# Where a group's sums of squares and its first output pieces stand among the projections: a Mamba-2 / HGRN2 trunk on one Trainium2 core

## The chip, the core and the metric

The program runs on one core of one Trainium2 chip. The metric is device time in microseconds (us). The core has five engines with a queue each: TensorE (PE in the profile, its weight loads PEld), VectorE (DVE), ScalarE (ACT), GpSimd (POOL) and SyncE (SP, which here only issues transfers). An engine takes its instructions in the order of its queue; engines wait for each other by semaphores.

## The reference, cut to what matters

Two layers on 512 tokens of width 1024. The first one's token mixer is a Mamba-2 SSD, and the change lies in it. Its last steps are a gated output, a norm over each of 4 groups of 512 channels, and a projection:

```python
zxbcdt = u @ w_in
xbc = silu(causal_depthwise_conv(xbc, conv_w, conv_b))
...
y = y_diag + y_off + d_skip * xs
y = y.reshape(bsz, seq, SSD_D_INNER) * silu(z)
y = rms_norm(y.reshape(bsz, seq, g_, SSD_D_INNER // g_), norm_w)
return y.reshape(bsz, seq, SSD_D_INNER) @ w_out
```

What follows (layer norm, squared-ReLU MLP, a gated embedding, then the second layer with an HGRN2 mixer) is not touched.

## The kernel before, in words

Products in float32 are made of three float32r products each: every operand is split into a high part (`whi`, a cast on ScalarE, `L110`) and a low part (`wlo`, a subtraction on VectorE, `L112`), and `mm3` (`L116` to `L118`) adds high x high, low x high and high x low. A weight unit of 128 x 1024 is loaded into one of 3 buffers `raw`, then split into one of 6 buffers `whi` and one of 6 `wlo`; so the cast of a later unit waits until TensorE has done with the unit that had its buffer.

The 2048 channels of the SSD are 16 tiles of 128 channels, 4 to a group. `x_part(j)` projects tile j (24 matmuls into a bank of PSUM), and `conv_silu` makes `xs` of it: a start on ScalarE (`L570`), three steps on VectorE (`L573`), silu on ScalarE (`L574`). `z_part(j)` projects its gate and applies silu (`L622`). `decays`, `states`, `turn_pair` and `mixed` are the scan: decay products `m` (`L663`, exp `L668`, product with `cbm` `L669`) and `cd` (`L656`), a pair's states by matmul (`L679`), a pair's transposes (`L639`), and the output `py` (`L696`, `L698`). `finish(j, ...)` gates the output, splits it into `ys[g]` and adds its square to `ss[g]` (`L724`).

A loop over rounds k = 1 to 8 takes the tiles in pairs. Round k projects tiles 2k and 2k+1 and mixes the pair before, 2k-2 and 2k-1. So group 0's fourth square is added at the end of round 2, group 1's in round 4, group 2's in round 6. In rounds 3, 5 and 7 `rms_group` sums the squares over the channels with four float32 matmuls against a matrix of 1/512 (`L729`, the sums), takes the root on ScalarE (`L731`) and the reciprocal on VectorE (`L732`): `ri`. The group's part of the output projection comes in 8 pieces of 12 matmuls (`out_part`, 4 token chunks by 2 halves of the width); VectorE scales a piece by `ri` and adds it to `acc` (`L250`). `some(n)` puts the next n pieces into the queue, and the table `PIECES` says how many stand in a round before its second projection (`mine`) and how many behind it (`theirs`). Group 2's pieces come in round 8.

TensorE's order is the order of the code (`manual_schedule`). The orders of the other queues are made by a scheduler when the program is built, from the same code and its priorities. Four banks of PSUM (`psj`, `pj` in names) go round among projections, sums and pieces: a matmul that is the first to write a bank waits until its last reader is done.

Of the kernel before, what the change touches and what calls it, by code (L numbers as in the profile page):

```python
# [41 lines left out]
def trunk(ctx: ExitStack, tc, a):  # L42
# [11 lines left out]
    psj = pool("psj", 4, space=PSUM)  # L54
# [10 lines left out]
    def mk(p, shape, tag, dt=F32, **kw):  # L65
        return p.tile(list(shape), dt, tag=tag, name=nm(tag), **kw)
# [22 lines left out]
    def bank(p, tag):  # L89
        return mk(p, [P, T], tag)  # L90
# [8 lines left out]
    def unit(src, lead=LEAD):  # L99
        n = src.shape[1]  # L100
        with tc.high_priority(offset=lead):
            raw = mk(raws, [P, 1024], "raw")
            nc.sync.dma_start(raw[:, :n], src)
        return split(raw[:, :n], lead)
# [133 lines left out]
    def out_part(units, n, xs, c, h, first, scale, last=False, sums=None):  # L238


        sl = slice(c * P, (c + 1) * P)
        ps = bank(psj, "pj")
        for k in range(n):
            hi, lo = units[k // 2]
            ks = slice((k % 2) * 512, (k % 2 + 1) * 512)
            mm3(ps, xs.h(k, sl), xs.l(k, sl), hi[:, ks], lo[:, ks], k == 0, k == n - 1)
        d = acc[:, c, h * 512 : (h + 1) * 512]
        with tc.high_priority(offset=SOON if last else 0):
            if scale is not None:
                nc.vector.scalar_tensor_tensor(d, ps, scale[:, c : c + 1], d, ALU.mult, ALU.add)  # L250
            elif sums is not None:
                nc.vector.tensor_tensor_reduce(d, ps, d, 1.0, 0.0, ALU.add, ALU.add, sums[:, c, h : h + 1])
            elif first:
                nc.vector.scalar_tensor_tensor(d, d, ALPHA, ps, ALU.mult, ALU.add)
            else:
                nc.vector.tensor_add(d, ps, d)
# [301 lines left out]
    def dt_tail():  # L558

        pt = bank(psm, "pm")  # L560
        for i, src in enumerate((dt, wt, cs)):
            nc.tensor.transpose(pt[:, i * P : (i + 1) * P], src, ident)
        t = mk(cpool, [P, 3, NCH, 32], "toks")
        nc.vector.tensor_copy(t, pt[:, : 3 * P].rearrange("p (i c h) -> p i c h", i=3, c=NCH))
        return [t[:, i] for i in range(3)]
# [20 lines left out]
    def bc_group(g):  # L586
        bcm = []
        for which in range(2):
            ps = projected(10 * g + which)
            t = tmp(("bm", "cm")[which], [P, T])  # L590
            conv_silu(ps, 16 + 4 * which + g, t)
            bcm.append(t)
        return bcm

    def bc_prep(bcm, pt, pc):
        bm, cm = bcm
        for c in range(3):
            nc.tensor.transpose(pt[:, c * P : (c + 1) * P], bm[:, c * P : (c + 1) * P], ident)
        btok = tmp("btok", [P, 3, P])
        nc.scalar.copy(btok, pt[:, : 3 * P].rearrange("p (c n) -> p c n", c=3))  # L600
        for c in range(NCH):
            sl = slice(c * P, (c + 1) * P)
            nc.tensor.matmul(pc[:, sl], bm[:, sl], cm[:, sl], start=True, stop=True)
        cbm = tmp("cbm", [P, T])
        nc.vector.tensor_mul(
            cbm.rearrange("p (c l) -> p c l", c=NCH), pc.rearrange("p (c l) -> p c l", c=NCH), bc(triu, 1, NCH)
        )
        return btok, cbm, cm
# [4 lines left out]
    def x_part(j):  # L613
        ps = projected(10 * (j // 4) + 2 + 2 * (j % 4))
        xs = tmp("xs", [P, T])
        conv_silu(ps, j, xs)
        live[j] = [xs]

    def z_part(j):
        ps = projected(10 * (j // 4) + 3 + 2 * (j % 4))  # L620
        sz = tmp("sz", [P, T])
        nc.scalar.activation(sz, ps, AF.Silu)  # L622
        if j in live:
            live[j].insert(1, sz)
        return sz

    def load_decay(j):
        csb = mk(w4, [P, 2, T], "a")
        nc.sync.dma_start(csb, bass.AP(tensor=csd.tensor, offset=csd.offset + 2 * j * T, ap=[[0, P], [T, 2], [1, T]]))
        decay[j] = csb  # L630

    def turn_pair(k, pts):
        dt_tok, w_tok, cs_tok = toks
        xw = tmp("xw", [P, 3, 2, 2, 64])
        pair[k] = [xw, mk(sm, [P, 2, 2, NCH], "cd")]
        for t, pt in enumerate(pts):
            xs = live[2 * k + t][0]
            for c in range(NCH):
                nc.tensor.transpose(pt[:, c * P : (c + 1) * P], xs[:, c * P : (c + 1) * P], ident)  # L639
        views = [pt.rearrange("p (c h q) -> p c h q", c=NCH, h=2) for pt in pts]  # L640
        for t, v in enumerate(views):
            j = 2 * k + t
            nc.vector.tensor_mul(xw[:, :, t], v[:, 0:3], bc(w_tok[:, 0:3, 2 * j : 2 * j + 2], 3, 64))
        for t, v in enumerate(views):
            j = 2 * k + t
            xdt = tmp("xdt", [P, NCH, 2, 64])
            nc.vector.tensor_mul(xdt, v, bc(dt_tok[:, :, 2 * j : 2 * j + 2], 3, 64))
            live[j].append(xdt)
# [77 lines left out]
    def rms_group(g, pr):  # L726

        for c in range(NCH):
            nc.tensor.matmul(pr[:, 64 * c : 64 * c + 64], ss[g][:, c * P : (c + 1) * P], ones_s, start=True, stop=True)  # L729
        ri = mk(sm, [P, NCH], "ri")  # L730
        nc.scalar.activation(ri, pr[:, : 64 * NCH].rearrange("p (c n) -> p c n", c=NCH)[:, :, 0], AF.Sqrt, bias=eps)  # L731
        nc.vector.reciprocal(ri, ri)  # L732
        return ri

    def pieces(g, ri):

        for h in range(2):
            units = [unit(a["wso"][4 * g + 2 * h + i]) for i in range(2)]
            for c in range(NCH):
                out_part(units, 4, ys[g], c, h, False, ri)  # L740
                yield

    outs = iter(())
    bcm = {}

    def some(n):
        for _ in range(n):
            next(outs)

    PIECES = {3: (2, 2), 4: (2, 2), 5: (2, 2), 6: (2, 2)}  # L750

    with tc.manual_schedule(engines={mybir.EngineType.PE}):
        bcm[0] = bc_group(0)
        for j in range(2):
            load_decay(j)
            x_part(j)
            z_part(j)
        prep[0] = bc_prep(bcm[0], bank(pst, "pt"), bank(psy, "py0"))
        toks.extend(dt_tail())
        turn_pair(0, (bank(psy, "py1"), bank(psj, "pj")))  # L760
        for k in range(1, 9):
            i, j = 2 * k, 2 * k + 1
            mine, theirs = PIECES.get(k, (0, 0))
            decays(i - 2)
            if k < 8:
                if k in (4, 6):
                    bcm[k // 2] = bc_group(k // 2)
                x_part(i)
            else:
                finish(13, *held[:2], z_part(13))  # L770
                z_part(14)
            states(k - 1)
            if k in (3, 5, 7):
                outs = pieces(k // 2 - 1, rms_group(k // 2 - 1, bank(psj, "pj")))
            decays(i - 1)
            some(mine)
            if k < 8:
                load_decay(i)
                x_part(j)
                load_decay(j)  # L780
            some(theirs)
            if k == 1:
                bcm[1] = bc_group(1)
            elif k < 7:
                z_part(i - 2)
                z_part(i - 1)
            elif k == 7:
                z_part(12)
            else:
                z_part(15)  # L790
                some(4)
            if k == 2:
                nc.sync.dma_start(acc, a["x"])
                for c in range(NCH):
                    nc.vector.tensor_scalar(acc[:, c, :], acc[:, c, :], ALPHA, None, ALU.mult)
            done = [mixed(i - 2), (mixed(i - 1))] if k != 7 else [mixed(12)]
            if k == 7:
                live[13].insert(1, None)
                held = mixed(13)
            if k < 8:  # L800
                if k % 2 == 0:
                    prep[k // 2] = bc_prep(bcm[k // 2], bank(psj, "pj"), bank(psj, "pj"))
                turn_pair(k, (bank(pst, "pt"), bank(psm, "pm")))
            for t, d in enumerate(done):
                finish(i - 2 + t, *d)
        some(4)
# [494 lines left out]
```

## Time and profile before

| | us |
|---|---|
| timed runs | 1434.31, 1432.96, 1432.22; median 1432.96 |
| the profiled execution | 1434.46 |
| its span on the core | 1432.4 |
| TensorE busy | 1417.2 (99%) |
| VectorE, ScalarE busy | 1023.5 (71%), 738.7 (52%) |
| TensorE waiting for VectorE's `L724` before `L729` | 6.9 in 3 waits |

A row of the timeline gives start, length, engine, line, operation, out<-in, shapes, how many instructions it merges, and in brackets the idle time before it with what ended it. A float32 matmul stands there as two records, so the four matmuls of the sums are x8. PEclk in a row of a stretch is the clock that TensorE was granted, 1.00 for full speed. The profiled execution's own time is 2.06 us more than its span.

### The profile page before, as it was taken

How to read it: one execution, taken by the hardware profiler on the slowest of the kernel's cores; microseconds unless marked ns; L12 is line 12 of the kernel's file. 1: busy time of each engine (PE TensorE's matmuls, PEld its weight loads, DVE VectorE, ACT ScalarE, POOL GpSimd, SP SyncE). 2: the span in 40 equal slices, each digit the busy share in tenths (PEclk: the TensorE clock that was granted, in tenths of full speed). 3: DMA queues.
4: the chain of work that ended last, by engine and by line, in shares of the span. 5: the costliest groups of instructions: out<-in, count | busy, mean ns of one | idle time of the engine just before them, and what ended most of it. 6: DMA issues, size and time to landing. Idle time of an engine off the chain costs nothing.

```text
span 1432.4 us, 20277 instructions
## 1 busy us (share of the span) xinstructions
PE 1417.2 (99%) x8063; PEld 1183.9 (83%) x8063; DVE 1023.5 (71%) x1673; ACT 738.7 (52%) x1085; POOL 1.6 (0%) x9
## 2 busy tenths in 40 slices
PE   9999999999999999999999999999999999999998
PEld 7887878878888888888888888888898888888887
DVE  7996876696966768676874674766795867667873
ACT  7884655574255454445543445464455454543641
POOL 0000000000000000000000000000000000000000
PEclk9999999999999999999999999999999999999999
DMA  7423223322533444443422232222163444434231
GB/s 289 169 98 103 104 90 117 108 98 104 177 117 118 147 132 147 140 140 131 134 95 84 75 103 90 79 85 90 47 244 107 147 135 145 147 132 162 89 118 44
DMA packets 48958, 174.81 MB, mean 122 GB/s; under 512 B 5728, under 2 KB 6368, under 8 KB 48736
## 3 DMA queue, kind: packets, MB, share of 16 engines
q1 hardware_dynamic: 48864, 173.52, 35.6%
q8 instruction: 63, 1.03, 0.3%
q14 instruction: 31, 0.25, 0.1%
HBM read 171.34 MB, written 2.16 MB: 121 GB/s over the span
## 4 chain that ended last, share of the span: by engine, by line
PE 92%; DVE 5%; ACT 1%; DMA 1%; issue 0%; SPq 0%; ACTq 0%
PE pj L116 24%; PE pj L117 24%; PE pj L118 24%; PE py L116 5%; PE py L117 5%; PE py L118 5%; PE py L960 1%; PE py L696 1%; DMA acc<-in_x 1%; DVE wlo L112 1%; PE py L698 0%; PE pt L230 0%; DMA acc<-in_xw 0%; PE pm L230 0%; ACT whi L110 0%
## 5 line engine op out<-in xcount | busy, mean ns | idle before, releaser
L110 ACT CAST whi<-raw 128x1024 fp32r<-128x1024 f32 x226 | 237.1, 1051 | 404.0 <-PE pj L117 277.6
L112 DVE TENSOR_TENSOR wlo<-raw,whi 128x1024 fp32r<-128x1024 f32 x226 | 275.0, 1221 | 206.6 <-ACT whi L110 200.6
L116 PE MATMUL pj<-b,whi 128*128 128x512 f32 (+1 forms) x1008 | 380.5, 378 | 0.2 <-ACT b L235 0.2
L117 PE MATMUL pj<-b,whi 128*128 128x512 f32 (+1 forms) x1008 | 378.9, 376 | 0.7 <-DVE b L236 0.7
L118 PE MATMUL pj<-b,wlo 128*128 128x512 f32 (+1 forms) x1008 | 378.7, 376 | 0.0
L118 PE MATMUL pj<-whi,b 128*128 128x512 f32 (+1 forms) x592 | 230.2, 389 | 0.0
L116 PE MATMUL pj<-whi,b 128*128 128x512 f32 (+1 forms) x584 | 229.8, 394 | 0.1
L117 PE MATMUL pj<-wlo,b 128*128 128x512 f32 (+1 forms) x584 | 227.0, 389 | 0.0
L117 PEld LDWEIGHTS pj<-b,whi 128*128 128x128 f32 x1008 | 189.7, 188 | 34.8 <-DVE b L236 0.9
L118 PEld LDWEIGHTS pj<-b,wlo 128*128 128x128 f32 x1008 | 189.7, 188 | 34.7
L116 PEld LDWEIGHTS pj<-b,whi 128*128 128x128 f32 x1008 | 189.5, 188 | 34.7 <-ACT b L235 0.5
L118 PEld LDWEIGHTS pj<-whi,b 128*128 128x128 f32 x592 | 111.8, 189 | 22.9 <-DVE b L1155 0.2
L116 PEld LDWEIGHTS pj<-whi,b 128*128 128x128 f32 x584 | 110.5, 189 | 23.3 <-ACT k L889 0.5
L117 PEld LDWEIGHTS pj<-wlo,b 128*128 128x128 f32 x584 | 110.5, 189 | 21.6
L110 ACT CAST whi<-r 128x1024 fp32r<-128x1024 f32 x64 | 67.1, 1049 | 65.0 <-PE pj L118 36.8
L112 DVE TENSOR_TENSOR wlo<-r,whi 128x1024 fp32r<-128x1024 f32 x64 | 78.1, 1220 | 21.8 <-ACT whi L110 21.8
L118 PE MATMUL py<-whi,b 128*128 128x512 f32 x216 | 84.1, 390 | 0.0
L117 PE MATMUL py<-wlo,b 128*128 128x512 f32 x192 | 74.7, 389 | 0.0
L116 PE MATMUL py<-whi,b 128*128 128x512 f32 x192 | 74.4, 389 | 0.0
L573 DVE SCALAR_TENSOR_TENSOR cv<-pj,cst,cv 128x509 f32<-128x509 f32 (+2 forms) x66 | 48.9, 743 | 2.8 <-ACT cv L570 2.4
L118 PEld LDWEIGHTS py<-whi,b 128*128 128x128 f32 x216 | 40.5, 188 | 8.5
L116 PEld LDWEIGHTS py<-whi,b 128*128 128x128 f32 x192 | 36.0, 188 | 7.6
(335 smaller groups left out, 1808.0 us busy)
## 6 DMA issues: line engine op xcount, KB each, us to landing
raw<-in_w SPq DMA_DIRECT2D x112, 512.0 KB, 3.3
r<-in_w SPq DMA_DIRECT2D x64, 512.0 KB, 3.4
raw<-in_wssd SPq DMA_DIRECT2D x38, 512.0 KB, 4.0
a<-csd SPq DMA_DIRECT2D x16, 512.0 KB, 3.6
raw<-in_wso SPq DMA_DIRECT2D x16, 512.0 KB, 3.4
raw<-in_wg SPq DMA_DIRECT2D x16, 512.0 KB, 3.3
raw<-in_whvg SPq DMA_DIRECT2D x16, 512.0 KB, 3.4
raw<-in_whq SPq DMA_DIRECT2D x16, 512.0 KB, 3.3
```

Source lines behind the costliest of these rows:

```text
L110: nc.scalar.copy(hi[:, :n], f)
L112: nc.vector.tensor_sub(lo[:, :n], f, f32(hi[:, :n]))
L116: nc.tensor.matmul(out, sh, mh, start=start, stop=False, **kw)
L117: nc.tensor.matmul(out, sh, ml, start=False, stop=False, **kw)
L118: nc.tensor.matmul(out, sl, mh, start=False, stop=stop, **kw)
L573: nc.vector.scalar_tensor_tensor(cv[:, d:], ps[:, : T - d], convw[:, i, k : k + 1], cv[:, d:], ALU.mult, ALU.add)
L696: nc.tensor.matmul(yd[64 * r : 64 * r + 64, sl], xdt[:, c, r, :], m[:, r, sl], start=True, stop=c == 0)
L960: nc.tensor.matmul(ps[r][32 * b : 32 * b + 32, base + n * c : base + n * c + n], kk[r][:, ts], moving(r, 4 * c + b), start=True, stop=True,)
```

## The change

The sums and the iterator over the pieces are made behind the second projection of rounds 3, 5 and 7 instead of behind `states`, and in rounds 3 and 5 the table puts four pieces behind that projection and none before it. Rounds 4 and 6 keep two and two, round 8 is as it was.

```diff
-    PIECES = {3: (2, 2), 4: (2, 2), 5: (2, 2), 6: (2, 2)}
+    PIECES = {3: (0, 4), 4: (2, 2), 5: (0, 4), 6: (2, 2)}
...
             states(k - 1)
-            if k in (3, 5, 7):
-                outs = pieces(k // 2 - 1, rms_group(k // 2 - 1, bank(psj, "pj")))
             decays(i - 1)
             some(mine)
             if k < 8:
                 load_decay(i)
                 x_part(j)
                 load_decay(j)
+            if k in (3, 5, 7):
+                outs = pieces(k // 2 - 1, rms_group(k // 2 - 1, bank(psj, "pj")))
             some(theirs)
```

On TensorE in round 3, before: the states of pair 2 (`pt`, `pm`), the sums into `pj_1078`, and the first piece into `pj_1112`, whose stationary operand `b` is the gated output `ys`.

```order
L679 MATMUL pt_1067<-xw_981,btok_971 128x256 x2
L679 MATMUL pm_1068<-xw_981,btok_971 128x256
L729 MATMUL pj_1078<-ones_s_169,ss_734 128x64 x4
L116 MATMUL pj_1112<-whi_1102,b_115_727 128x512
L117 MATMUL pj_1112<-wlo_1104,b_115_727 128x512
L118 MATMUL pj_1112<-whi_1102,b_116_728 128x512
```

And now, the same place in the code's order of sums and first piece: the last matmuls of the second projection (tile 7, `pj_1094`), the sums into `pj_1134`, and the first piece into `pj_1154`.

```order
L116 MATMUL pj_1094<-b_6_112,whi_1097 128x512
L117 MATMUL pj_1094<-b_8_114,whi_1097 128x512
L118 MATMUL pj_1094<-b_6_112,wlo_1099 128x512
L729 MATMUL pj_1134<-ones_s_169,ss_734 128x64 x4
L116 MATMUL pj_1154<-whi_1144,b_115_727 128x512
L117 MATMUL pj_1154<-wlo_1146,b_115_727 128x512
L118 MATMUL pj_1154<-whi_1144,b_116_728 128x512
```

The sums no longer follow the float32 matmuls of the states; they stand between float32r matmuls on both sides, and the projection follows the states. Three pieces (`pj_1168`, `pj_1182`, `pj_1196`) follow the first one. In the built program the second waits for the last convolution step of the first projection, the third for the root (`L731`), the fourth for the last convolution step of the second projection.

On ScalarE in round 3, before, behind the square of tile 3 (`sq_1010`): the root `ri`, the silu of tile 6 (`xs_1060`), an exp, `cd`, the cast of a later weight unit (`whi_1398`) and the convolution's start of tile 7 (`cv_1174`).

```order
L720 ACTIVATE sq_1010<-y_1005 128x512
L731 ACT_TABLE_LOAD
L731 ACTIVATE ri_1083<-pj_1078,cst_165 128x4
L574 ACT_TABLE_LOAD
L574 ACTIVATE xs_1060<-cv_1061 128x512
L668 ACT_TABLE_LOAD
L668 ACTIVATE b_1086<-b_1086 128x1024
L656 ACTIVATE cd_1309<-a_1180 128x8
L110 CAST whi_1398<-raw_1396 128x1024
L570 ACTIVATE cv_1174<-pj_1142,cst_165 128x512
```

And now, where tile 7's convolution is `cv_1126`:

```order
L720 ACTIVATE sq_1010<-y_1005 128x512
L110 CAST whi_1398<-raw_1396 128x1024
L570 ACTIVATE cv_1126<-pj_1094,cst_165 128x512
L574 ACT_TABLE_LOAD
L574 ACTIVATE xs_1060<-cv_1061 128x512
L668 ACT_TABLE_LOAD
L668 ACTIVATE b_1078<-b_1078 128x1024
L731 ACT_TABLE_LOAD
L731 ACTIVATE ri_1139<-pj_1134,cst_165 128x4
L656 ACT_TABLE_LOAD
L656 ACTIVATE cd_1309<-a_1132 128x8
```

The root went from first to behind the cast, the convolution's start, silu and exp. The cast waits for the second projection's last matmul with a high weight, because `whi_1398` takes the buffer of `whi_1097`. In round 5 the order is the same but for the convolution's start, which stands behind the exp.

On ScalarE in round 7, before, from the exp to the silu of the second projection's tile, 15 (`xs_2605`); `sz_2645` is the gate of tile 12:

```order
L668 ACTIVATE b_2558<-b_2558 128x1024
L570 ACTIVATE cv_2606<-pj_2574,cst_165 128x512
L656 ACTIVATE cd_2680<-a_2612 128x8
L110 CAST whi_2860<-raw_2858 128x1024
L110 CAST whi_2968<-raw_2966 128x1024
L622 ACT_TABLE_LOAD
L622 ACTIVATE sz_2645<-pj_2614 128x512
L574 ACTIVATE xs_2605<-cv_2606 128x512
```

And now, where it is `xs_2597`; the cast `whi_2860`, the silu of tile 14 and its table load, and the exp's table load stand ahead of the first row:

```order
L668 ACTIVATE b_2550<-b_2550 128x1024
L570 ACTIVATE cv_2598<-pj_2566,cst_165 128x512
L731 ACT_TABLE_LOAD
L731 ACTIVATE ri_2611<-pj_2606,cst_165 128x4
L622 ACT_TABLE_LOAD
L622 ACTIVATE sz_2645<-pj_2614 128x512
L656 ACT_TABLE_LOAD
L656 ACTIVATE cd_2680<-a_2604 128x8
L574 ACT_TABLE_LOAD
L574 ACTIVATE xs_2597<-cv_2598 128x512
```

The root and three table loads came between exp and that silu. On TensorE, `L639` transposes `xs_2597` behind the mixing of tiles 12 and 13.

## Prediction

> **What bounds the kernel now.** I read the page first, then TensorE's waits, then the stretches around each wait with the granted clock. TensorE is busy for 99% of the span, and in the SSD stage it waits for one thing only: `L729`, the matmuls that add up a group's sums of squares. The columns of the wait are total us, times, longest.
>
> ```profile
> PE 1417.2 (99%) x8063; PEld 1183.9 (83%) x8063; DVE 1023.5 (71%) x1673; ACT 738.7 (52%) x1085; POOL 1.6 (0%) x9
> ```
> ```profile
> PE pj L729 <- DVE ss L724: 6.9, 3, 3.0
> ```
>
> Next, six of the stretches of 3.41 us: start and end, length, busy time of TensorE, weight loads, VectorE, ScalarE and GpSimd, then PEclk.
>
> ```profile
> 108.34:111.75 3.41, 1.48 (x11) 1.42 (x12) 3.41 (x8) 1.87 (x3) 0.00 (x0) 1.00 0.00 0
> 111.75:115.16 3.41, 3.41 (x10) 2.63 (x9) 3.41 (x12) 2.09 (x3) 0.00 (x0) 0.51 0.00 0
> ...
> 200.49:203.90 3.41, 1.45 (x9) 0.97 (x7) 3.41 (x8) 3.39 (x5) 0.00 (x0) 1.00 0.00 0
> 203.90:207.31 3.41, 3.41 (x13) 2.93 (x13) 3.41 (x11) 1.39 (x3) 0.00 (x0) 0.51 0.00 0
> ...
> 292.64:296.05 3.41, 2.17 (x10) 1.51 (x8) 3.41 (x7) 2.73 (x4) 0.00 (x0) 1.00 0.00 0
> 296.05:299.46 3.41, 2.69 (x16) 2.39 (x17) 3.41 (x8) 1.68 (x3) 0.00 (x0) 1.00 0.00 0
> ```
>
> A wait costs more than its length here. After a stretch in which TensorE was busy for 1.48 or 1.45 us, the next stretch ran at 0.51; after 2.17 and 2.69 it did not. The two lowered stretches lie 92.15 us apart, 27 times 3.413, so I read them as steps of one fixed grid: a grid step with 1.93 us or more of idleness costs half the clock for the next step, one with up to 1.24 us costs nothing. A lowered step costs 3.41 x 0.49 = about 1.65 us.
>
> **What is removed.** TensorE's rows at the three places, from the last states matmul to the first matmul behind the moved work (start, length, line; 129.17, 222.44 and 312.84 start a z projection). In round 3:
>
> ```profile
> 106.69 0.59 PE L679 MATMUL pm<-xw,btok 128*128 128x256 f32 x2
> 110.27 1.08 PE L729 MATMUL pj<-ones_s,ss 128*128 128x64 f32 x8 [2.98 <-DVE ss L724]
> 111.15 0.48 PE L116 MATMUL pj<-whi,b 128*128 128x512 f32 x1
> 111.47 0.39 PE L117 MATMUL pj<-wlo,b 128*128 128x512 f32 x1
> ...
> 123.73 0.39 PE L116 MATMUL pj<-whi,b 128*128 128x512 f32 x1
> ...
> 129.17 0.39 PE L116 MATMUL pj<-b,whi 128*128 128x512 f32 x1
> ```
>
> In rounds 5 and 7:
>
> ```profile
> 200.95 0.59 PE L679 MATMUL pm<-xw,btok 128*128 128x256 f32 x2
> 203.50 1.57 PE L729 MATMUL pj<-ones_s,ss 128*128 128x64 f32 x8 [1.96 <-DVE ss L724]
> ...
> 222.44 0.39 PE L116 MATMUL pj<-b,whi 128*128 128x512 f32 x1
> ```
> ```profile
> 294.21 0.59 PE L679 MATMUL pm<-xw,btok 128*128 128x256 f32 x2
> 296.77 1.10 PE L729 MATMUL pj<-ones_s,ss 128*128 128x64 f32 x8 [1.96 <-DVE ss L724]
> 297.68 0.47 PE L116 MATMUL pj<-b,whi 128*128 128x512 f32 x1
> ...
> 303.25 0.39 PE L116 MATMUL pj<-b,whi 128*128 128x512 f32 x1
> ...
> 308.78 0.66 PE L696 MATMUL py<-b,xdt 128*64 128x128 f32 x8
> ...
> 311.99 0.66 PE L639 MATMUL pt<-cst,xs 128*128 128x128 f32 x4
> 312.48 0.60 PE L639 MATMUL pm<-cst,xs 128*128 128x128 f32 x4
> 312.84 0.48 PE L116 MATMUL pj<-b,whi 128*128 128x512 f32 x1
> ```
>
> Before therefore spends 22.48 us (129.17 - 106.69), 21.49 us and 18.63 us there.
>
> **What after spends, on TensorE alone.** A projection straight behind states is in round 1, where no sums stand between:
>
> ```profile
> 78.11 0.59 PE L679 MATMUL pm<-xw,btok 128*128 128x256 f32 x2
> 78.35 0.58 PE L116 MATMUL pj<-b,whi 128*128 128x512 f32 x1
> ...
> 84.00 0.39 PE L116 MATMUL pj<-b,whi 128*128 128x512 f32 x1
> ```
>
> So the second projection starts 0.24 us behind states and takes 5.65 us. The sums have had their data by 110.27, 203.50 and 296.77 (their starts now); in after their turn comes at 106.69 + 5.89 = 112.58, at 206.84 and at 300.10, so the old waits go. The sums take 0.88 us (110.27 to 111.15), two pieces 5.44 us (123.73 to 129.17), so 2.72 each, and the first matmul behind the sums 0.09 us more than the usual 0.23. This is also the cost of the "run of their own": the projection behind states starts slowly (0.2 us), as the one behind the sums did before, and both are in these rows. Rounds 3 and 5, without any new wait: 0.24 + 5.65 + 0.88 + 0.09 + 4 x 2.72 = 17.74 us.
>
> What else moves is hidden: on SyncE's queue the second projection's weight load changes places with the pieces' two, three slots for the same three loads in their order of use, all cast a round ahead; GpSimd's queue is the same. On ScalarE the new order alternates functions more often and has one table load more in rounds 3 and 5 each and two in round 7.
>
> **The new wait of rounds 3 and 5.** Four pieces in a row need four of the pool's four banks. In the built program the third piece waits for ScalarE's square root, which reads the bank of the sums, and the fourth for the second projection's third convolution step on VectorE. ScalarE's queue there (its order in round 3 above): the cast of a weight unit into the second projection's buffer, the convolution's start, then a table load and silu, a table load and exp, a table load and the square root. Before, the square root was first. The prices:
>
> ```profile
> 111.38 0.26 ACT L731 ACTIVATE ri<-pj,cst 128x4 f32<-128x4 f32 x1 [1.42 <-PE pj L729]
> 113.04 1.28 ACT L574 ACT_TABLE_LOAD   x1 [1.39 <-DVE ri L732]
> ...
> 116.27 1.06 ACT L668 ACTIVATE b<-b 128x1024 f32<-128x1024 f32 x1
> ...
> 123.70 1.05 ACT L110 CAST whi<-raw 128x1024 fp32r<-128x1024 f32 x1 [5.41 <-PE pj L117]
> 124.66 0.78 ACT L570 ACTIVATE cv<-pj,cst 128x512 f32<-128x512 f32 x1
> ```
>
> The cast started 0.03 us before the projection's successor (123.73), so call the projection's end E: cast and convolution start end at E + 1.71 (123.70 to 125.44), table load to end of exp takes 4.29 (113.04 to 117.33), table load and square root 1.28 + 0.26, gaps 0.05: E + 7.6. TensorE stands before the third piece at E + 0.88 + 2.81 + 2.72 = E + 6.41. A wait of 1.2 us, in both rounds. At under 1.24 us it leaves the clock alone by the rows. The fourth piece: exp ends at E + 6.0, then VectorE runs one m product, one convolution step, the reciprocal, one weight subtraction and the last step:
>
> ```profile
> 119.16 1.21 DVE L669 TENSOR_TENSOR b<-b,cbm 128x1024 f32<-128x1024 f32 x1
> 120.29 1.22 DVE L112 TENSOR_TENSOR wlo<-raw,whi 128x1024 fp32r<-128x1024 f32 x1
> ...
> 127.32 1.53 DVE L573 SCALAR_TENSOR_TENSOR cv<-pj,cst,cv 128x510 f32<-128x510 f32 x2
> ```
>
> 1.2 + 1.2 + 1.5 + 0.1 = 4.0 at most, E + 10.0; the fourth piece stands at E + 7.6 + 2.72 = E + 10.3. Covered, barely; if the subtraction slips, it costs that much. Round 3: 22.48 - 17.74 - 1.2 = 3.5 us gained. Round 5: 21.49 - 18.94 = 2.5 us.
>
> **The new wait of round 7.** No pieces follow; behind the sums come one z projection (5.57, 297.68 to 303.25, and 0.1 into the mixing), two mixings (3.21, 308.78 to 311.99) and the first half of the turn (0.49). The second half transposes what silu makes of the second projection. That projection starts 3.2 us earlier than before (294.21 + 0.24 = 294.45 for 297.68), but in ScalarE's order of round 7 the root and three table loads now come between the exp and this silu. The missing prices:
>
> ```profile
> 304.91 0.21 ACT L656 ACTIVATE cd<-a 128x8 f32<-128x8 f32 x1 [0.18 <-DMA a<-csd]
> ...
> 311.02 0.60 ACT L622 ACTIVATE sz<-pj 128x512 f32<-128x512 f32 x1
> 311.51 0.62 ACT L574 ACTIVATE xs<-cv 128x512 f32<-128x512 f32 x1
> ```
>
> With E = 300.10: cast to E + 1.0, table load to exp E + 5.3, convolution start E + 6.0, table load and square root E + 7.5, table load and z silu E + 9.4, table load and cd E + 10.9, table load and silu E + 12.8 = 312.9. TensorE is there at E + 0.88 + 5.67 + 3.21 + 0.49 = 310.35. A wait of 2.6 to 2.7 us, and the z projection starts 0.36 us later (312.48 to 312.84), at 313.4 instead of 312.84: 0.6 us lost, the old wait of 2.2 and more exchanged for a later one.
>
> **The clock.** The 2.5 us of idleness in round 7 lies on an unknown phase of the grid. If 1.93 us in one step are needed, 60% of the phases give them (27% have no boundary inside, and 46% of the rest leave a part that long); if just over 1.24 are enough, all do. I take a lowered step, 1.6 us. [...]
>
> **Sum.** 3.5 + 2.5 - 0.6 - 1.6 = 3.8 us off the profiled execution's 1434.46, 1430.7. Behind this stage TensorE has no wait above 1 us, so I carry the gain to the end. The profiled execution stands 1.5 us above the runs' median of 1432.96. That may be the profiling (then 1429.2 for a median run) or one lowered step that a median run doesn't pay (then 1430.7); I take 1429.9.
>
> **Rivals.** A, the forecast, 1429.2 to 1430.7: 45%. B, the round-7 wait lowers no step, for its phase on the grid or because short gaps don't lower it as a rule: 1.6 less, 1427.6 to 1429.1: 20%. [...] C, ScalarE gets through faster than I walked it and no new wait appears: 1.2 + 1.2 + 2.7 + 1.6 less, 1422.5 to 1424.0: 6%; against it, each load in the queue has its row. D, the new waits are longer by a few tenths, so each of the three holds enough idleness and lowers the clock: 1434.46 - 5.4 + 4.9 = 1434.0, or 1432.5 on the median's scale, no change: 20%. E, slower: the row of four runs out of banks, and the third piece waits until VectorE has emptied the first (behind the last convolution step, about E + 10.6 instead of E + 7.6). Then rounds 3 and 5 wait 3.0 us more each, 6.0, and three steps are lowered: 1434.46 - 5.4 + 6.0 + 4.9 = 1440.0, or 1438.5. It decides as soon as that bank is the one handed out; for it speaks that VectorE was busy through 3.41 of 3.41 us in the quoted stretches, against it that the program's waits name the square root. With any other backlog of that size: 9%.
>
> 0.2% of the time, 2.9 us, is about what a measurement of this kernel can tell from no change: faster means below 1430.1, slower above 1435.8. A is split 25 to 20 by that line: faster 25 + 20 + 6 = 51%, same 20 + 20 = 40%, slower 9%. The range leaves out C, E and a few per cent at B's and D's far ends: 1427.0 to 1434.0.
>
> **What would show it.** Right: no TensorE wait at `L729`; waits of 1.0 to 1.3 us at the third piece (`L116`) of rounds 3 and 5, released by ScalarE `L731`; one of about 2.5 us at `L639` in round 7, released by ScalarE `L574`; at most one step at 0.51. Wrong: a wait left at `L729` (the sums' data come later than now), waits released by VectorE `L573` or `L250` at the pieces, or new waits outside the SSD stage.

## The result, and the profile after

| | before | after |
| --- | --- | --- |
| median, us | 1434.65 (8 runs, 1432.22 to 1435.57) | 1429.88 (8 runs, 1428.67 to 1430.94) |
| profiled execution, us | 1434.46 | 1430.54 |
| its span, us | 1432.4 | 1428.5 |

The ratio after to before is 0.9969 (95% interval 0.9959 to 0.9978). That is faster by 0.3%: small, but the interval leaves out 1. The three runs of before in the first table were on the low side: with the five taken beside the changed kernel the median is 1434.65, close to the profiled execution.

TensorE's waits of the changed kernel (total us, times, longest):

```profile
PE pm L639 <- ACT xs L574: 2.7, 1, 2.7
PE pj L116 <- ACT ri L731: 2.2, 2, 1.1
```

`L729`, which led this view before with 6.9 us, is gone. In its place stand the two new waits: the third piece twice, the second half of round 7's turn once. 6.9 us of waits became 4.9.

TensorE's rows at the three places (start, length, line), from the last states matmul to the first matmul behind the moved work. Rounds 3 and 5:

```profile
106.13 0.59 PE L679 MATMUL pm<-xw,btok 128*128 128x256 f32 x2
112.03 1.00 PE L729 MATMUL pj<-ones_s,ss 128*128 128x64 f32 x8
112.84 0.48 PE L116 MATMUL pj<-whi,b 128*128 128x512 f32 x1
119.68 0.50 PE L116 MATMUL pj<-whi,b 128*128 128x512 f32 x1 [1.12 <-ACT ri L731]
125.25 0.39 PE L116 MATMUL pj<-b,whi 128*128 128x512 f32 x1
```
```profile
197.03 0.59 PE L679 MATMUL pm<-xw,btok 128*128 128x256 f32 x2
210.56 0.50 PE L116 MATMUL pj<-whi,b 128*128 128x512 f32 x1 [1.10 <-ACT ri L731]
216.17 0.39 PE L116 MATMUL pj<-b,whi 128*128 128x512 f32 x1
```

The sums now start without a wait, and so do the first, second and fourth piece; the third waits 1.12 and 1.10 us. States to z projection takes 19.12 us (125.25 - 106.13) and 19.14 us, where it took 22.48 and 21.49.

Round 7:

```profile
287.95 0.59 PE L679 MATMUL pm<-xw,btok 128*128 128x256 f32 x2
...
306.86 0.66 PE L639 MATMUL pm<-cst,xs 128*128 128x128 f32 x4 [2.69 <-ACT xs L574]
307.27 0.48 PE L116 MATMUL pj<-b,whi 128*128 128x512 f32 x1
```

From states to the z projection it takes 19.32 us now and took 18.63: 0.69 us lost. And the wait of 2.69 us has a consequence, which the stretches around it show (start and end, length, busy time of TensorE, weight loads, VectorE, ScalarE and GpSimd, PEclk):

```profile
304.40:307.90 3.50, 1.04 (x7) 0.95 (x8) 3.46 (x14) 3.46 (x6) 0.00 (x0) 1.00 0.00 0
307.90:311.30 3.40, 3.40 (x10) 2.64 (x9) 3.40 (x8) 3.37 (x5) 0.00 (x0) 0.51 0.06 18
```

The clock in the second stretch is 0.51: one lowered step behind the wait. No stretch of rounds 3 and 5 of this profile is below 1.00.

The two profiles can now be closed against each other. TensorE reaches round 3 0.56 us earlier than before (106.13 for 106.69), a difference that arose ahead of all changed code: it is there already behind the states of round 1 (77.55 for 78.11). Then 22.48 - 19.12 = 3.36 and 21.49 - 19.14 = 2.35 are gained, 0.69 and one step of 3.41 x 0.49 = 1.65 lost: 0.56 + 3.36 + 2.35 - 0.69 - 1.65 = 3.93 us. The spans differ by 3.9 us. Nothing behind round 7 gives any of it back.

### The profile page after: what moved, and what is told of

The parts are those of the page before. It is cut to its first block, busy times and chain, and to the rows that moved or that the text cites. A ratio compares the mean times of both kernels' runs of the same rounds, so it can differ in the third digit from the quotient of the medians.

```text
span 1428.5 us, 20283 instructions
## 1 busy us (share of the span) xinstructions
PE 1415.3 (99%) x8063; PEld 1182.2 (83%) x8063; DVE 1023.1 (72%) x1673; ACT 743.9 (52%) x1089; POOL 1.6 (0%) x9
## 4 chain that ended last, share of the span: by engine, by line
PE 93%; DVE 3%; ACT 2%; DMA 1%; issue 0%; SPq 0%; DVEq 0%; ACTq 0%
PE pj L116 24%; PE pj L117 24%; PE pj L118 24%; PE py L116 5%; PE py L117 5%; PE py L118 5%; PE py L696 1%; PE py L960 1%; DVE wlo L112 1%; PE py L698 1%; DMA a<-csd 1%; PE pt L679 0%; PE pt L230 0%; DMA acc<-in_xw 0%; PE pm L230 0%
```

## The experiments

My theory: the gain of rounds 3 and 5 is real and reduced by a wait for ScalarE's root; round 7 loses, through ScalarE's order of work and through the clock step that its wait brings on. Times of runs below are medians beside the kernel before on the same chip.

### Rounds 3 and 5 alone, round 7 alone

Round 7's sums are set back behind the states:

```diff
+            if k in (7,):
+                outs = pieces(k // 2 - 1, rms_group(k // 2 - 1, bank(psj, "pj")))
...
-            if k in (3, 5, 7):
+            if k in (3, 5):
```

> The moved sums in rounds 3 and 5 alone; round 7 keeps its sums and first pieces behind the states, as before. My theory: rounds 3 and 5 show the rows of the changed kernel (no wait at L729, 1.1 us at the third piece) and give about 6 us; round 7 gets its old wait of 1.96 us at the sums back, and loses the 2.7 us wait at L639 with its lowered clock step. That returns 0.6 us and, where the old wait does not lower the clock either, some 1.2 to 1.6 us more: about 1428.5 (1428 to 1429.9), ratio to the kernel before 0.9957. Rival, that round 7's move is a gain like the other two (2.5 us): about 1432.4, ratio 0.998.

Measured: 1429.28 us (9 runs) beside 1434.09; ratio 0.9969 (0.9956 to 0.9982). The profile, of a run of 1428.08, has the old wait of 1.96 us and none at `L639`, and no lowered step in its whole span:

```profile
PE pj L116 <- ACT ri L731: 2.2, 2, 1.1
PE pj L729 <- DVE ss L724: 2.0, 1, 2.0
```

The converse moves the sums in round 7 alone, and leaves the table of pieces as it was:

```diff
-    PIECES = {3: (0, 4), 4: (2, 2), 5: (0, 4), 6: (2, 2)}
+    PIECES = {3: (2, 2), 4: (2, 2), 5: (2, 2), 6: (2, 2)}
...
+            if k in (3, 5):
+                outs = pieces(k // 2 - 1, rms_group(k // 2 - 1, bank(psj, "pj")))
...
-            if k in (3, 5, 7):
+            if k in (7,):
```

> The moved sums in round 7 alone; rounds 3 and 5 and the table of pieces as before. My theory: the two old waits at L729 in rounds 3 and 5 stay, the wait at L639 in round 7 becomes 2.7 us and is followed by a step at half clock: 0.6 us lost and up to 1.6 us more where the old 1.96 us wait had not lowered the clock: 1434.5 to 1436.5, ratio to the kernel before 1.000 to 1.0013. Rival, that the move in round 7 is a gain like the other two (2.5 us): about 1432.2, ratio 0.9983.

Measured: 1435.67 us (12 runs) beside 1434.09; ratio 1.0016 (1.0005 to 1.0026). Slower, as the theory had it and a little more. The waits:

```profile
PE pj L729 <- DVE ss L724: 4.9, 2, 3.0
PE pm L639 <- ACT xs L574: 2.7, 1, 2.7
```

So rounds 3 and 5 carry the whole gain, and the move in round 7 by itself costs about 1.6 us. In the first of the two kernels the old 1.96 us wait of round 7 is back. Three of its nine runs have a granted clock of 1.000, four 0.999 and two 0.997, and they reach from 1427.09 to 1431.41 us, so its median shows less than its profile, which is of a run at 1.000. A clock of 0.997 is more than one lowered step, since one, 3.41 us at 0.50, is 0.0012 of the mean clock; where these fell, the one profile cannot show.

### What the wait in round 7 costs by itself

```diff
+            for _ in range(9 if (k, t) == (7, 1) else 0):
+                nc.tensor.matmul(pt[:, 0:P], ident, ident, start=True, stop=True)
```

> The changed kernel with nine more float32 matmuls of 128x128 (some 2 us of work, into a bank that the next ones overwrite) between the two halves of round 7's turn, where TensorE waits 2.7 us. They change no result and no wait's end. My theory: the wait at L639 shrinks to about 0.7 us, its end stays where it was (the silu of tile 15), no step at half clock follows, and the time falls by the 1.6 us of that step in most runs: about 1428.7, the profile's z projection in round 7 without spacings of 0.43 us. Rival one, that the wait's length alone costs: 1429.9, no change. Rival two, that work on TensorE there delays something: above 1430.5.

Measured: 1428.95 us (10 runs), ratio 0.9967 (0.9956 to 0.9977). TensorE in the profile (the fillers have `L639`, the turn `L641`):

```profile
307.30 0.66 PE L641 MATMUL pm<-cst,xs 128*128 128x128 f32 x4 [0.69 <-ACT xs L574]
```

The wait's end is where it was, and the clock stays at 1.00 behind it. How far TensorE has come after the z projection and the next one shows what that is worth. The sums and the next states, in the changed kernel and with the fillers:

```profile
293.85 1.00 PE L729 MATMUL pj<-ones_s,ss 128*128 128x64 f32 x8
319.90 1.02 PE L679 MATMUL pt<-xw,btok 128*128 128x256 f32 x4
```
```profile
294.28 1.00 PE L731 MATMUL pj<-ones_s,ss 128*128 128x64 f32 x8
318.72 1.02 PE L681 MATMUL pt<-xw,btok 128*128 128x256 f32 x4
```

The turn's second half starts 13.02 us behind the sums (307.30 - 294.28), for 13.01 in the changed kernel (306.86 - 293.85). The next states start 24.44 us behind them, for 26.05: 1.61 us saved, all of it behind the wait. The whole time would not have settled this: the median is 0.9 us under the changed kernel's, the ratio nearly the same.

The same test on the kernel before, where three waits had stood:

```diff
+        for _ in range(7 if g < 3 else 0):
+            nc.tensor.matmul(pr[:, 0:P], ident, ident, start=True, stop=True)
```

> The kernel before with seven more float32 matmuls of 128x128 (1.54 us of work, into the bank of the sums, overwritten by them) ahead of the sums in rounds 3, 5 and 7, where TensorE waited 2.98, 1.96 and 1.96 us. The waits' ends stay. My theory: the waits at L729 shrink to about 1.4 and 0.4 us, no step at half clock follows them, and what the lowered steps had cost comes off, two of 1.65 us in the profiled execution of before: about 1431.4, ratio to the kernel before 0.9977. Rival, that the waits alone cost and the clock nothing: no change, ratio 1.000.

Measured: 1430.78 us (11 runs) beside 1433.80; ratio 0.9982 (0.9973 to 0.9991). The sums start no earlier in this kernel: in round 3, 3.58 us behind the last states matmul (109.97 - 106.39), as before (110.27 - 106.69), and in round 5 it is 2.56 us for 2.55. So the 3.0 us came off without any wait ending sooner, and the granted clock went up with it: 8 of these 11 runs have 0.999 or 1.000, of the 15 of before beside them only three. What is left as the cause is the clock. That is more than half of what the change itself brings, without moving any needed instruction. One part of the expectation failed: the profiled run still shows a lowered step in round 3. The last states matmul and the wait there, then the stretches around it:

```profile
106.39 0.59 PE L679 MATMUL pm<-xw,btok 128*128 128x256 f32 x2
109.97 1.07 PE L731 MATMUL pj<-ones_s,ss 128*128 128x64 f32 x8 [1.43 <-DVE ss L724]
```
```profile
107.77:111.18 3.41, 1.98 (x17) 1.78 (x17) 3.41 (x9) 1.97 (x4) 0.00 (x0) 1.00 0.00 0
111.18:114.59 3.41, 3.41 (x10) 2.64 (x9) 3.41 (x12) 2.01 (x3) 0.00 (x0) 0.50 0.00 0
```

Here a step with 1.43 us of idleness was followed by one at 0.50; in another profile a step with 1.61 us was followed by one at 1.00, as the last section shows.

### Whom the third piece waits for

ScalarE's root and its reciprocal for the first two groups are put ahead of the silu in the scheduler's order:

```diff
+        with tc.high_priority(offset=60 if g < 2 else 0):
+            nc.scalar.activation(ri, pr[:, : 64 * NCH].rearrange("p (c n) -> p c n", c=NCH)[:, :, 0], AF.Sqrt, bias=eps)
+            nc.vector.reciprocal(ri, ri)
```

> The changed kernel with ScalarE's root (L731) and its reciprocal of the first two groups set ahead of the next silu in the scheduler's order; TensorE's order is untouched. My theory: the wait of 1.1 us at the third piece goes in rounds 3 and 5, since the bank of the sums is read some 2 us sooner; round 7 is as in the changed kernel, 2.7 us at L639: about 1427.7, 2.2 us under the changed kernel, ratio to the kernel before 0.995. Rival, that the third piece waits for something else (VectorE's emptying of the first): wait and time stay, 1429.9.

Measured: 1427.14 us (6 runs) beside 1434.09; ratio 0.9960 (0.9945 to 0.9975). ScalarE in round 3 of the changed kernel, and of this one:

```profile
112.00 1.04 ACT L110 CAST whi<-raw 128x1024 fp32r<-128x1024 f32 x1 [3.90 <-PE pj L117]
...
116.98 1.06 ACT L668 ACTIVATE b<-b 128x1024 f32<-128x1024 f32 x1
118.07 1.28 ACT L731 ACT_TABLE_LOAD   x1
119.36 0.26 ACT L731 ACTIVATE ri<-pj,cst 128x4 f32<-128x4 f32 x1
```
```profile
111.79 1.04 ACT L110 CAST whi<-raw 128x1024 fp32r<-128x1024 f32 x1 [3.90 <-PE pj L117]
112.85 1.28 ACT L732 ACT_TABLE_LOAD   x1
114.14 0.26 ACT L732 ACTIVATE ri<-pj,cst 128x4 f32<-128x4 f32 x1
```

From the start of the cast to the end of the root it was 7.62 us (119.62 - 112.00) and is 2.61. The wait at the third piece is gone, and none takes its place. TensorE in round 3, last states matmul, first piece and z projection:

```profile
105.92 0.59 PE L679 MATMUL pm<-xw,btok 128*128 128x256 f32 x2
...
112.62 0.48 PE L116 MATMUL pj<-whi,b 128*128 128x512 f32 x1
...
123.62 0.39 PE L116 MATMUL pj<-b,whi 128*128 128x512 f32 x1
```

17.70 us; the prediction had summed up 17.74 for a round without any wait. The rival of the expectation, VectorE's emptying of the first piece, is not ruled out by this run, because the reciprocal came earlier too, and with it the emptying: it starts at 115.66 here. The changed kernel's own trace rules it out. There VectorE empties the first piece only from 121.74 on, after the third piece had started at 119.68, 0.06 us behind the root's end:

```profile
121.74 2.06 DVE L250 SCALAR_TENSOR_TENSOR acc<-pj,ri,acc 128x512 f32<-128x512 f32 x3
```

The other half of that question is whether it is four pieces in a row that make the wait:

```diff
-    PIECES = {3: (0, 4), 4: (2, 2), 5: (0, 4), 6: (2, 2)}
+    PIECES = {3: (0, 2), 4: (4, 2), 5: (0, 2), 6: (4, 2)}
```

> The changed kernel with two pieces behind the sums in rounds 3 and 5 instead of four (the other six go into rounds 4 and 6). My theory: it isn't the row of four that waits but whoever takes the bank of the sums two banks later: now the z projection's first matmul, with the same 1.1 us wait for the root, so the time is like the changed kernel's, 1429.9 (1429 to 1431). Rival, that the row of four makes the wait: the wait is gone and the time 1427.7.

Measured: 1428.17 us (5 runs) beside 1433.80; ratio 0.9961 (0.9948 to 0.9975). The time is under what I had expected, because one of the two waits is gone:

```profile
PE pj L116 <- ACT ri L731: 1.1, 1, 1.1
```

The one that stays is in round 5, at the z projection:

```profile
208.55 0.50 PE L116 MATMUL pj<-b,whi 128*128 128x512 f32 x1 [1.11 <-ACT ri L731]
```

ScalarE in rounds 3 and 5 of this kernel:

```profile
111.41 1.04 ACT L110 CAST whi<-raw 128x1024 fp32r<-128x1024 f32 x1 [3.90 <-PE pj L117]
...
114.45 0.26 ACT L731 ACTIVATE ri<-pj,cst 128x4 f32<-128x4 f32 x1
```
```profile
200.89 1.04 ACT L110 CAST whi<-raw 128x1024 fp32r<-128x1024 f32 x1 [3.90 <-PE pj L117]
...
208.23 0.26 ACT L731 ACTIVATE ri<-pj,cst 128x4 f32<-128x4 f32 x1
```

The scheduler had put the root first in round 3 (ending 3.30 us behind the cast's start) and left it behind silu and exp in round 5 (7.60 us). With the root early there is no wait; with the root late the next taker of its bank waits 1.11 us, though only two pieces stand ahead of it and it is a z projection. So the length of the row is not the cause. My expectation was wrong about round 3's order, which I hadn't read in the built program, and right about the mechanism.

### Whom round 7 waits for

The convolution and silu of tile 15 are put ahead of the root, the gate and the decays:

```diff
-        conv_silu(ps, j, xs)
+        with tc.high_priority(offset=60 if j == 15 else 0):
+            conv_silu(ps, j, xs)
```

> The changed kernel with the convolution and silu of tile 15 (L570 to L574) set ahead of the root, the gate and the decays in the scheduler's order; TensorE's order is untouched. My theory: round 7's wait of 2.7 us at L639 goes, since its silu now ends about 3 us sooner, and with it the step at half clock: 2.7 and 1.2 to 1.6 us, so about 1426.0, ratio to the kernel before 0.994; rounds 3 and 5 keep 1.1 us at the third piece. Rival, that what stands behind the silu on ScalarE (root, gate, decays) is waited for at the same place or in round 8: a wait of 2 us or more by another name, and 1429 to 1430.5.

Measured: 1425.38 us (5 runs, 1425.11 to 1425.67) beside 1433.80; ratio 0.9945 (0.9932 to 0.9957). ScalarE in round 7 of the changed kernel and of this one, from the cast to the silu that the turn transposes:

```profile
293.82 1.05 ACT L110 CAST whi<-raw 128x1024 fp32r<-128x1024 f32 x1 [3.90 <-PE pj L117]
...
302.74 0.60 ACT L622 ACTIVATE sz<-pj 128x512 f32<-128x512 f32 x1
...
304.88 1.28 ACT L574 ACT_TABLE_LOAD   x1
306.18 0.63 ACT L574 ACTIVATE xs<-cv 128x512 f32<-128x512 f32 x1
```
```profile
293.49 1.05 ACT L110 CAST whi<-raw 128x1024 fp32r<-128x1024 f32 x1 [3.90 <-PE pj L117]
...
301.12 1.28 ACT L574 ACT_TABLE_LOAD   x1
302.42 0.63 ACT L574 ACTIVATE xs<-cv 128x512 f32<-128x512 f32 x1
302.95 0.58 ACT L623 ACTIVATE sz<-pj 128x512 f32<-128x512 f32 x1
```

The silu now shares the gate's table and ends 9.56 us behind the cast's start, not 12.99. TensorE has no wait left in round 7, and all five runs show a granted clock of 1.000. From states to the z projection it takes 16.42 us:

```profile
287.61 0.59 PE L680 MATMUL pm<-xw,btok 128*128 128x256 f32 x2
...
304.03 0.48 PE L116 MATMUL pj<-b,whi 128*128 128x512 f32 x1
```

With that order the move gains in round 7 too: 18.63 - 16.42 = 2.2 us instead of a loss.

### Both orders

> The two orders of ScalarE's work together: the root of the first two groups earlier, and the silu of tile 15 earlier. My theory: the two gains add, since they lie in different rounds: 2.2 and 3.9 us under the changed kernel, about 1423.8, ratio to the kernel before 0.9925; no wait above 1 us at the pieces or at round 7's turn. Rival, that the waits pass to the next bank: 1427 or more.

Measured: 1422.67 us (5 runs, 1422.09 to 1423.75) beside 1433.80; ratio 0.9927 (0.9914 to 0.9939). Against the changed kernel's median the root's order brought 2.7 us, the silu's 4.5 and both 7.2 us; reckoned each from the runs of before beside it, 2.2, 3.7 and 6.4. Either way they add to within half a microsecond, as things in different rounds should. The rows say the same: 19.12 - 17.70 = 1.42 us in each of two rounds, and 19.32 - 16.42 = 2.90 with a lowered step of 1.65. This is the fastest of all versions, faster than both kernels of the case. Both orders are close to those that the kernel before had: there too the root stood first in round 3, and the gate and this silu shared a table in round 7. So the move with these orders is worth 11.1 us, and as it was built 4.8. The longest wait that TensorE has left in it is the one at the very start, outside the rounds:

```profile
PE pm L150 <- DVE y L147: 1.0, 1, 1.0
```

## Why the prediction came out right

Forecast 1429.9, measured 1429.88. The mechanism was right, step by step; that the number agrees to 0.02 us is luck. The forecast stood on the low three-run median, 1432.96, and took 3.1 us off it; the eight runs have 1434.65, and the medians differ by 4.8 us. The base was 1.7 us too low and the gain 1.7 us too small. Point by point:

- **The old waits at `L729` go.** Right in all three rounds.
- **Rounds 3 and 5 take 18.94 us.** They take 19.12 and 19.14. The part without waits was right (17.74 forecast, 17.70 in the kernel whose root is early), and the wait at the third piece is 1.12 and 1.10 us for 1.2, with ScalarE's root as its releaser. The wait costs 0.3 us more than the row gives for it: the four pieces with it take 12.41 us (125.25 - 112.84), with the early root 11.00, so 1.41 for a wait of 1.12. Of that, 0.13 is a slow restart (5.57 us for the two pieces behind the wait, for 5.44), and 0.16 that a row's idle time begins at the end of a matmul (0.39) where the next would have started after 0.23.
- **The fourth piece is barely covered.** It doesn't wait; the cover held.
- **Round 7 waits 2.6 to 2.7 us for the silu of tile 15.** 2.69 us, and 0.69 us lost for 0.6. (The prediction's own sum gives 312.9 - 310.35 = 2.55.) The walk through ScalarE's queue, one table load after the other, gave E + 12.8 for the end of that silu; the trace has 306.81 - 293.85 = E + 12.96.
- **The clock: one lowered step, 1.6 us.** Right in the profiled execution. That 1.93 us of idleness in a step is enough and 1.24 harmless was my estimate, read from four stretches of one profile. The runs show no such limit: 1.43 us was followed by a step at 0.50 in one profile and 1.61 us by one at 1.00 in another (last section). So the range of 60% to all phases is an estimate still, and that this execution got its step may in part be the luck of the phase.
- **Sum 3.8 us.** 3.9 between the two profiled executions, but the start-up's 0.56 us helps: without it 3.37. What was missed are the three rounds: 0.18, 0.20 and 0.09 us, each to the bad.
- **The choice between 1429.2 and 1430.7.** This one came out well for a reason other than mine. I had asked whether the profiled run's 1.5 us over the median were the profiling or a step. Over the 39 runs of before beside the experiments, the span goes with the granted clock: 1428.2 us on average at 1.000 (4 runs), 1429.9 at 0.999 (4), 1431.5 at 0.998 (14), 1433.2 at 0.996 (14); the other three, at 0.997 and 0.995, fit in. One step is 0.0012 of the mean clock, so each costs about 1.67 us; and the profiled run, with two, was an ordinary one; it was the three-run median that was low. The mean span of the 39 is 1431.8 and of the changed kernel's eight runs 1427.8: 4.0 us, close to the 3.8 of the sum; the means of the two kernels' eight runs, taken side by side, differ by 4.5. Why these differ is not known.

Rival C fell with the waits themselves, and E because the third piece started before VectorE had begun to empty the first. B may be true of a part of the runs: six of the eight have a clock of 0.998 and a mean span of 1428.2 us, two have 0.999 and 1426.7, which would fit one step less, but no profile of such a run was taken. Its second ground, that short gaps don't lower the clock, is not shown: 1.43 us was followed by 0.50. D was nearer than its rows made it look: waits of 1.12 us lowered nothing in any profile here, and 1.43 us did in one, so three tenths more might have changed the result by two steps.

## What to carry to other kernels

When work is moved so that TensorE's wait goes, walk the queues of the engines that serve the next buffers, instruction by instruction with the table loads counted: here the walk gave both new waits to within 0.15 us, and the orders that remove them (root first, silu beside the gate that shares its table) brought 6.4 to 7.2 us where the move as it was built had brought 4.8. Price a wait with its effect on the clock, as read from the stretches behind it: in the kernel before, the steps with 1.88 and 1.96 us of idleness were each followed by one at 0.50, an estimated 1.65 us on top, and filling the changed kernel's wait of 2.69 us saved 1.61 us. And a median of three runs whose spread comes from such steps is not a base for a fraction of a per cent.

## What the hardware showed beyond that

- Less idleness than 1.93 us was followed by a lowered step once: in the kernel before with fillers it was 1.43 us in one step of 3.41 us, and the next ran at 0.50. But in the kernel with both orders a step with 1.61 us of idleness (busy 1.80), in pieces of 0.89, 0.24 and 0.74 us that partly reach over its ends, was not. Counted back from its lowered step at 1419.5 by whole steps of 3.4133 us (the two lowered steps of the kernel before start at 111.80 and 203.96, 27 such lengths apart), it is this one, with the next:

```profile
381.87:385.28 3.41, 1.80 (x12) 1.39 (x12) 3.41 (x5) 1.07 (x2) 0.00 (x0) 1.00 0.42 154
385.28:388.70 3.42, 3.37 (x28) 3.37 (x29) 3.35 (x4) 0.44 (x1) 0.00 (x0) 1.00 0.00 0
```

  Counted so in the kernel before, the steps from 108.39 and 200.54 have 1.88 and 1.96 us of idleness, and the next ran at 0.50; the one from 292.71 has 1.31 us, and the next ran at 1.00. In the changed kernel the step from 304.55 has 2.31 us, and the next ran at 0.50; the one from 389.88 has 1.20 us, and the next ran at 1.00. Five more lowered steps lie ahead of the end of three other profiles (three with round 7 alone, one with the root earlier, one with two pieces in a row), each behind 1.8 to 2.6 us of idleness, as far as stretches of 1 us tell. What decides is open.
- The step does not fall in every run of a program: four of the 39 runs of before have a granted clock of 1.000, though a wait of 2.98 us stands in the one profile of that program. Whether the wait was shorter in those runs, fell on two steps, or was let pass is open.
- A lowered step behind the last matmul costs TensorE nothing, but counts in a run's mean clock. In the kernel with both orders, TensorE's last matmul starts at 1416.76, and the clock falls behind it (stretches as above):

```profile
1416.76 0.28 PE L118 MATMUL pj<-whi,b 128*128 128x256 f32 x1
```
```profile
1420.00:1421.00 1.00, 0.00 (x0) 0.00 (x0) 0.00 (x0) 0.00 (x0) 0.00 (x0) 0.50 0.00 0
```

  So a mean clock of 0.999 can mean a step that was paid or one that was not; only the stretches of a profile tell them apart.
- From exp to the root, ScalarE spends the 1.28 us of the table load and some 0.04 us of gaps: exp ends at 118.04 in the changed kernel, the load starts at 118.07, the root at 119.36. Of the changed kernel's 66 loads between other work of ScalarE, 58 have less than 0.05 us of idle time on either side. The 1.39 us ahead of the silu's load at 113.04 in the kernel before is a wait that VectorE ended.
